# Seven block products in place of eight in part of the down projections of a two-FFN encoder block

## The chip, the cores and the metric

The kernel runs on one core of a Trainium2 chip. The metric is the device time of one execution, in microseconds; three runs of the kernel before gave 2103.3 to 2103.77 us, median 2103.62 us. The core has a matrix engine (TensorE, PE in the rows below), a vector engine (DVE), a scalar engine (ACT), GpSimd (POOL), a queue engine that issues transfers (SP), and 16 DMA engines.

## The reference, cut to what matters

```python
def swiglu(h, w_gate, w_up, w_down):
    return (jax.nn.silu(h @ w_gate) * (h @ w_up)) @ w_down

x = x + 0.5 * swiglu(rms_norm(x, norm_ffn1), ffn1_w_gate, ffn1_w_up, ffn1_w_down)
...   # mixer: sparse attention and a gated MLP on h = rms_norm(x)
x = x + 0.5 * swiglu(rms_norm(x, norm_ffn2), ffn2_w_gate, ffn2_w_up, ffn2_w_down)
```

x is 256 rows (SEQ) by 2048 columns (D_MODEL), the feed-forward width D_FF is 5632, everything float32. The down projection is therefore a product of 256 x 5632 with 5632 x 2048, and it occurs twice, once in each feed-forward block.

## The kernel before, in words

Every product is a sum over k-tiles of 128. `gemm` (L230 to L284) takes 1024 output columns at a time. For each pair of k-tiles one transfer on SP's queue brings 1 MB of weights into a buffer `w` (three buffers). For each k-tile `split_to` (L226 to L228) makes two parts of the 128 x 1024 weights: ACT casts them to the short matmul format (`wh`, L227), and DVE subtracts that from the original (`wl`, L228). There are three buffers of each. The activations were split in the same way before (`hTh`, `hTl` for the hidden layer). TensorE then does, for each of two row tiles t and two column halves j, three matmuls of 512 columns into one PSUM bank: high by high (L279), low by high (L280), high by low (L281). That is 12 matmuls for a k-tile, 24 for a pair.

`ffn` (L376 to L403) runs 11 chunks of 512 feed-forward columns: gate and up products over 16 k-tiles, SiLU on ACT (L389), product on DVE (L391), then a transpose through the DMA engines (`turn`, L291 to L299: planes on ACT, a transposing transfer, a copy on DVE) and a split into `hTh`, `hTl`. After all 11 chunks the down projection runs in two halves of 1024 columns, each over all 44 k-tiles, into four banks, which L401 adds to the residual `xres` with factor 0.5.

Side work such as the transposes stands in a queue `pending`; `tick` emits one piece after each k-tile. The order of instructions on each engine is fixed when the program is built, by a scheduler that follows a modelled timeline and the priorities of the code; at run time each engine works through its own list in order and waits at each instruction for what it needs. SP's queue is such a list too: a weight transfer waits until its buffer is free, and everything behind it waits with it.

Of the kernel before, what the change touches and what calls it, by code (L numbers as in the profile page):

```python
# [21 lines left out]
P = 128  # L22
# [44 lines left out]
def block_kernel(ctx: ExitStack, tc: tile.TileContext, x, positions, norm_ffn1, ffn1_w_gate, ffn1_w_up,  # L67
# [4 lines left out]
    const = ctx.enter_context(tc.tile_pool(name="const", bufs=1))  # L72
    act = ctx.enter_context(tc.tile_pool(name="act", bufs=1))
    wraw = ctx.enter_context(tc.tile_pool(name="wraw", bufs=3))
    wsp = ctx.enter_context(tc.tile_pool(name="wsp", bufs=3))
    tmp = ctx.enter_context(tc.tile_pool(name="tmp", bufs=8))
    small = ctx.enter_context(tc.tile_pool(name="small", bufs=4))
    psA = ctx.enter_context(tc.tile_pool(name="psA", bufs=6, space=bass.MemoryType.PSUM))
# [4 lines left out]
    def uid(s):  # L83
        cnt[0] += 1
        return f"{s}_{cnt[0]}"

    def ttile(shape=None):
        return tmp.tile(shape or [P, 512], F32, tag="t", name=uid("t"))
# [7 lines left out]
    def trbank(shape):  # L96
        return psT.tile(shape, F32, tag="tr", name=uid("tr"))
# [4 lines left out]
    def later(*stages):  # L102
        pending.extend(stages)
# [122 lines left out]
    def split_to(hi, lo, src):  # L226
        nc.scalar.copy(hi, src)  # L227
        nc.vector.tensor_sub(lo, src, hi.bitcast(F32))  # L228

    def gemm(xh, xl, nk, load, widths, first=0, rate=1, lead=None):  # L230
# [52 lines left out]
            k0 += kg  # L283
        return banks  # L284

    def loader(wap, c0, ncol):
        def load(k0, kg, dst):
            nc.sync.dma_start(dst, wap[k0 * P:(k0 + kg) * P, c0:c0 + ncol].rearrange("(k p) c -> p k c", p=P))
        return load
# [23 lines left out]
    class Normed:  # L313
# [59 lines left out]
        def xl(self, k, t):  # L373
            return self.l[:, k, t * P:(t + 1) * P]

    def ffn(nrm, wg, wu, wd, after_chunk, first=0, lead=None):  # L376
        with tc.tile_pool(name=uid("ffn"), bufs=1) as pool:
            hTh = pool.tile([P, KF, S], F32R, name=uid("hTh"))
            hTl = pool.tile([P, KF, S], F32R, name=uid("hTl"))
            for fc in range(FF // 512):  # L380
                def load(k0, kg, dst, fc=fc):
                    for i, wap in enumerate((wg, wu)):
                        nc.sync.dma_start(dst[:, :, i * 512:(i + 1) * 512],
                                          wap[k0 * P:(k0 + kg) * P, fc * 512:(fc + 1) * 512].rearrange(
                                              "(k p) c -> p k c", p=P))
                b = gemm(nrm.xh, nrm.xl, KD, load, [512, 512], first=first if fc == 0 else 0, lead=lead if fc == 0 else None)
                for t in range(NT):
                    sg = ttile()
                    nc.scalar.activation(sg, b[t][0], AF.Silu, scale=nrm.rstd[:, t:t + 1])  # L389
                    hh = ttile()  # L390
                    nc.vector.scalar_tensor_tensor(hh, b[t][1], nrm.rstd[:, t:t + 1], sg,  # L391
                                                   op0=ALU.mult, op1=ALU.mult)
                    later(partial(turn_split, hTh[:, fc * 4:fc * 4 + 4, t * P:(t + 1) * P],
                                  hTl[:, fc * 4:fc * 4 + 4, t * P:(t + 1) * P], hh))
            for half in range(2):
                b = gemm(lambda k, t: hTh[:, k, t * P:(t + 1) * P], lambda k, t: hTl[:, k, t * P:(t + 1) * P],
                         KF, loader(wd, half * 1024, 1024), [512, 512])
                for t in range(NT):
                    for j in range(2):
                        xs = xres[:, t, (half * 2 + j) * 512:(half * 2 + j + 1) * 512]  # L400
                        nc.vector.scalar_tensor_tensor(xs, b[t][j], 0.5, xs, op0=ALU.mult, op1=ALU.add)  # L401
                        if t == NT - 1 or after_chunk is to_out:
                            after_chunk(half * 2 + j, t)  # L403


    n1 = Normed(0)
# [387 lines left out]
```

## Time and profile before

| | |
|---|---|
| median of three runs | 2103.62 us |
| the profiled execution, its own time | 2102.13 us |
| its span (first to last instruction) | 2100.4 us |
| TensorE busy | 2084.0 us (99%), 9318 matmuls |
| DVE busy | 1165.4 us (55%) |
| ACT busy | 1038.5 us (49%) |
| weights and other data moved | 426.09 MB, mean 203 GB/s |

The profile is of one execution. Busy time of TensorE counts each matmul from its start to its modelled end; matmuls overlap, so the distance between starts says more than the duration of one. In the rows, "idle before" is the time an engine stood still ahead of a group of instructions, and the arrow names what released it. Idle time of an engine that is not the bottleneck costs nothing by itself.

### The profile page before, as it was taken

To read this page: it belongs to the slowest core of one execution; us is meant where nothing else is said; L and a number is where in the kernel's file an instruction comes from. 1 tells how busy PE (TensorE), PEld (TensorE's weight loads), DVE (VectorE), ACT (ScalarE), POOL (GpSimd) and SP (SyncE) were. 2 spreads that over 40 slices of the span, in tenths; PEclk is the share of its full clock that TensorE was granted. 3 is DMA by queue.
4 is the path that set the end of the run, shared out by engine and by line. 5 is a ranking of instruction groups with operands and counts; after the bars stand their busy time and mean duration, and the time that the engine had idled before them with its cause. 6 is when DMAs were issued, how large, how long until landed. Compare 5 with 4: busy or idle time off the path is not lost.

```text
span 2100.4 us, 24401 instructions
## 1 busy us (share of the span) xinstructions
PE 2084.0 (99%) x9318; PEld 1732.7 (82%) x9318; DVE 1165.4 (55%) x1362; ACT 1038.5 (49%) x1208; POOL 31.7 (2%) x60
## 2 busy tenths in 40 slices
PE   8999999999999999999999999999999999999998
PEld 6888888888888898888888888888888888888887
DVE  6555555555455457887544467555555555554443
ACT  5554444544345366567444445665444454443333
POOL 1000000000000000210000000000000000000000
PEclk9999999999999999999999999999999999999999
DMA  7666666666566477586665567676666666665654
GB/s 244 192 202 220 199 209 202 201 217 202 190 203 206 168 226 201 182 240 176 209 204 186 197 199 222 204 230 202 214 204 199 209 196 217 209 199 192 220 188 133
DMA packets 251526, 426.09 MB, mean 203 GB/s; under 512 B 106664, under 2 KB 108768, under 8 KB 251408
## 3 DMA queue, kind: packets, MB, share of 16 engines
q1 hardware_dynamic: 250880, 423.29, 63.7%
q0 software_dynamic: 528, 1.23, 0.3%
q8 instruction: 73, 1.20, 0.2%
q14 instruction: 45, 0.37, 0.1%
HBM read 398.26 MB, written 2.10 MB: 191 GB/s over the span
## 4 chain that ended last, share of the span: by engine, by line
PE 53%; ACT 0%; DMA 0%; DVE 0%; issue 0%; DVEq 0%
PE acc L279 17%; PE acc L281 17%; PE acc L280 17%; PE tr L687 0%; DMA tu<-pl 0%; DVE xres L401 0%; ACT L664 0%; PE tr L646 0%; ACT wh L227 0%; DVE pTs L299 0%; ACT vs L664 0%; DVEq L790 0%; ACT lgs L626 0%; ACT yah L227 0%; ACT pl L295 0%
## 5 line engine op out<-in xcount | busy, mean ns | idle before, releaser
L228 DVE TENSOR_TENSOR wl<-w,wh 128x1024 fp32r<-128x1024 f32 (+2 forms) x768 | 918.8, 1202 | 762.5 <-ACT wh L227 755.7
L227 ACT CAST wh<-w 128x1024 fp32r<-128x1024 f32 (+2 forms) x768 | 792.7, 1036 | 972.9 <-PE acc L280 957.3
L279 PE MATMUL acc<-wh,xTh 128*128 128x512 f32 (+1 forms) x2080 | 807.1, 388 | 3.4 <-ACT wh L227 3.4
L280 PE MATMUL acc<-wh,xTl 128*128 128x512 f32 (+1 forms) x2080 | 804.9, 387 | 0.0
L281 PE MATMUL acc<-wl,xTh 128*128 128x512 f32 (+1 forms) x2080 | 690.2, 387 | 0.0
L279 PEld LDWEIGHTS acc<-wh,xTh 128*128 128x128 f32 x2080 | 391.1, 188 | 81.8 <-ACT wh L227 4.7
L280 PEld LDWEIGHTS acc<-wh,xTl 128*128 128x128 f32 x2080 | 391.2, 188 | 76.6
L281 PEld LDWEIGHTS acc<-wl,xTh 128*128 128x128 f32 x2080 | 388.8, 188 | 77.3 <-DVE wl L228 0.6
L279 PE MATMUL acc<-wh,hTh 128*128 128x512 f32 x704 | 273.9, 389 | 0.0
L280 PE MATMUL acc<-wh,hTl 128*128 128x512 f32 x704 | 273.9, 389 | 0.0
L281 PE MATMUL acc<-wl,hTh 128*128 128x512 f32 x704 | 240.8, 389 | 0.0
L280 PEld LDWEIGHTS acc<-wh,hTl 128*128 128x128 f32 x704 | 132.2, 188 | 27.5
L281 PEld LDWEIGHTS acc<-wl,hTh 128*128 128x128 f32 x704 | 132.2, 188 | 27.4
L279 PEld LDWEIGHTS acc<-wh,hTh 128*128 128x128 f32 x704 | 132.2, 188 | 27.3
L299 DVE COPY t<-tu 128x1024 uint16<-128x1024 uint16 x60 | 45.6, 760 | 94.9 <-DMA tu<-pl 94.9
L295 ACT COPY pl<-t 128x1024 uint16<-128x1024 uint16 x58 | 60.4, 1043 | 0.4 <-DVE t L744 0.4
L280 PE MATMUL acc<-wh,ml 128*128 128x512 f32 x128 | 49.8, 389 | 0.0
L279 PE MATMUL acc<-wh,mh 128*128 128x512 f32 x128 | 49.6, 389 | 0.0
L281 PE MATMUL acc<-wl,mh 128*128 128x512 f32 x128 | 41.2, 389 | 0.0
L389 ACT ACTIVATE t<-acc,rstd 128x512 f32<-128x512 f32 x44 | 29.9, 690 | 10.7 <-PE acc L281 10.6
L391 DVE SCALAR_TENSOR_TENSOR t<-acc,rstd,t 128x512 f32<-128x512 f32 x44 | 32.0, 750 | 2.7 <-ACT t L389 2.7
L228 DVE TENSOR_TENSOR hTl<-t,hTh 128x512 fp32r<-128x512 f32 x44 | 30.2, 686 | 0.0
(182 smaller groups left out, 759.8 us busy)
## 6 DMA issues: line engine op xcount, KB each, us to landing
w<-in_ffn_w_down SPq DMA_DIRECT2D x88, 1024.0 KB, 5.1
w<-in_ffn_w_gate SPq DMA_DIRECT2D x175, 512.0 KB, 3.8
w<-in_ffn_w_up SPq DMA_DIRECT2D x175, 512.0 KB, 4.7
w<-in_w_in SPq DMA_DIRECT2D x72, 1024.0 KB, 5.0
w<-in_w_out SPq DMA_DIRECT2D x16, 1024.0 KB, 5.4
w<-in_w_in SPq DMA_DIRECT2D x16, 552.0 KB, 3.7
w<-in_w_up_attn SPq DMA_DIRECT2D x8, 1024.0 KB, 5.3
w<-in_w_up_sgu SPq DMA_DIRECT2D x8, 1024.0 KB, 5.4
```

Of the source, the lines that this page charges most:

```text
L227: nc.scalar.copy(hi, src)
L228: nc.vector.tensor_sub(lo, src, hi.bitcast(F32))
L279: nc.tensor.matmul(o_, sh, whj, start=(k == 0), stop=False)
L280: nc.tensor.matmul(o_, sl, whj, start=False, stop=False)
L281: nc.tensor.matmul(o_, sh, wlj, start=False, stop=(k == nk - 1))
L295: nc.scalar.copy(planes, src.bitcast(U16).rearrange("p (c h) -> p h c", h=2))
L299: nc.vector.tensor_copy(dst.bitcast(U16).rearrange("p j (c h) -> p h j c", h=2), turned)
L389: nc.scalar.activation(sg, b[t][0], AF.Silu, scale=nrm.rstd[:, t:t + 1])
L391: nc.vector.scalar_tensor_tensor(hh, b[t][1], nrm.rstd[:, t:t + 1], sg, op0=ALU.mult, op1=ALU.mult)
```

## The change

The feed-forward width is cut into two parts of 6 and 5 chunks (`PARTS`). For each part the gate and up products of its chunks run, and then the down projection over that part's k-tiles only (24 and 20), in two halves of 1024 columns. Each half ends with the four additions to `xres`, so there are twice as many of them.

In a half the k-tiles go in pairs. Of the 12 pairs of a half of the first part four (numbers 0, 2, 4, 6), and of the 10 pairs of the second part's halves four and two, are computed with seven block products instead of eight. The blocks are two row tiles by two k-tiles of activations and two k-tiles by two column halves of weights. The function that does it, `gemm_seven`, forms four sums or differences of weight blocks on DVE (three into a tile `T`, one in place in `w`), splits three tiles of 1024 columns and one of 512, and issues 7 x 3 = 21 matmuls. The sums of activation blocks S1 to S4 are made once per chunk by `sum_chunk`, which runs through the `pending` queue. The products P1, P5, P6 and P7 belong to several output blocks; after the last such pair `early` adds them to `xres` in five steps through the same queue. P2 and P3 collect in the two banks of the pool that otherwise serves transposes, P4 and a plain bank C22 in the main pool. The other pairs are computed as before, with 24 matmuls. The pool of split weights gets four buffers instead of three, and a scratch area for GpSimd's transfers is set to 4096 bytes.

Over the program each feed-forward block has 44 pairs in its halves, 14 of them with seven products.

```diff
-    wsp = ctx.enter_context(tc.tile_pool(name="wsp", bufs=3))
+    wsp = ctx.enter_context(tc.tile_pool(name="wsp", bufs=4))
...
+    def split_wide(src):
+        n = src.shape[-1]
+        whi = wsp.tile([P, 1024], F32R, tag="wh", name=uid("wh"))
+        wlo = wsp.tile([P, 1024], F32R, tag="wl", name=uid("wl"))
+        split_to(whi[:, :n], wlo[:, :n], src)
+        return [(whi[:, o:o + 512], wlo[:, o:o + 512]) for o in range(0, n, 512)]
+
+    def gemm_seven(tpool, xs, sums, nk, load, seven, early):
...
+        def product(name, st, w):
+            (sh, sl), (wh, wl) = st, w
+            if name not in acc:
+                acc[name] = trbank([P, 512]) if name in ("P2", "P3") else bank()
+            first = done[name] == 0
+            done[name] += 1
+            last = done[name] == total[name]
+            nc.tensor.matmul(acc[name], sh, wh, start=first, stop=False)
+            nc.tensor.matmul(acc[name], sl, wh, start=False, stop=False)
+            nc.tensor.matmul(acc[name], sh, wl, start=False, stop=last)
...
+            w = wraw.tile([P, 2048], F32, tag="w", name=uid("w"))
+            load(2 * g, 2, w.rearrange("p (k c) -> p k c", k=2))
+            if g in seven:
+                A11, A12, A22 = xs(2 * g, 0), xs(2 * g + 1, 0), xs(2 * g + 1, 1)
+                S1, S2, S3, S4 = sums(g)
+                T = tpool.tile([P, 3 * 512], F32, tag="T", bufs=2, name=uid("T"))
+                B11, B12, B21, B22 = (w[:, i * 512:(i + 1) * 512] for i in range(4))
+                nc.vector.tensor_sub(T[:, 0:512], B12, B11)
+                nc.vector.tensor_sub(B12, B22, B12)
+                nc.vector.tensor_add(T[:, 512:1024], B12, B11)
+                b11, t3 = split_wide(w[:, 0:1024])
+                product("P1", A11, b11)
+                product("P7", S3, t3)
+                t1, t2 = split_wide(T[:, 0:1024])
+                product("P5", S1, t1)
+                product("P6", S2, t2)
+                nc.vector.tensor_sub(T[:, 1024:1536], B21, T[:, 512:1024])
+                b21, b22 = split_wide(w[:, 1024:2048])
+                product("P2", A12, b21)
+                product("P3", S4, b22)
+                t4, = split_wide(T[:, 1024:1536])
+                product("P4", A22, t4)
...
+            else:
+                for kk in range(2):
+                    k = 2 * g + kk
+                    B = split_wide(w[:, kk * 1024:(kk + 1) * 1024])
+                    for t, names in enumerate((("P2", "P3"), ("P4", "C22"))):
+                        for j, name in enumerate(names):
+                            product(name, xs(k, t), B[j])
...
+                            pending.extendleft(reversed(early(acc["P1"], acc["P5"], acc["P6"], acc["P7"])))
+                    tick()
+        return [[acc["P2"], acc["P3"]], [acc["P4"], acc["C22"]]]
...
+    PARTS = ((0, 6, (4, 4)), (6, 5, (4, 2)))
+    KP = 24
...
+            for f0, nf, nseven in PARTS:
...
+                def sum_chunk(fi, fulls, hSh=hSh, hSl=hSl):
+                    f, g = fulls[0], fulls[1]
+                    s_ = ttile([P, 4, P])
+                    nc.vector.tensor_add(s_[:, 0, :], g[:, 0, :], g[:, 1, :])
+                    nc.vector.tensor_sub(s_[:, 1, :], s_[:, 0, :], f[:, 0, :])
+                    nc.vector.tensor_sub(s_[:, 2, :], f[:, 0, :], g[:, 0, :])
+                    nc.vector.tensor_sub(s_[:, 3, :], f[:, 1, :], s_[:, 1, :])
+                    split_to(hSh[:, fi], hSl[:, fi], s_)
...
+                    if fi < ns:
+                        later(partial(sum_chunk, fi, fulls))
...
+                    def early(P1, P5, P6, P7, c0=c0):
...
+                        def one():
+                            q["1"], q["5"] = ttile(), ttile()
+                            nc.scalar.activation(q["1"], P1, AF.Copy, scale=0.5)
+                            nc.scalar.activation(q["5"], P5, AF.Copy, scale=0.5)
+                            nc.vector.tensor_add(x0, q["1"], x0)
+
+                        def two():
+                            q["2"] = ttile()
+                            nc.vector.scalar_tensor_tensor(q["2"], P6, 0.5, q["1"], op0=ALU.mult, op1=ALU.add)
+                            nc.vector.tensor_add(x1, q["2"], x1)
+
+                        def three():
+                            q["3"] = ttile()
+                            nc.vector.scalar_tensor_tensor(q["3"], P7, 0.5, q["2"], op0=ALU.mult, op1=ALU.add)
+
+                        def four():
+                            nc.vector.tensor_add(both, both, q["3"][:, None, :].to_broadcast([P, 2, 512]))
+
+                        def five():
+                            nc.vector.tensor_add(right, right, q["5"][:, None, :].to_broadcast([P, 2, 512]))
...
+                    b = gemm_seven(pool, xs, sums, nf * 4, loader(wd[f0 * 512:(f0 + nf) * 512, :], c0, 1024),
+                                   [2 * i for i in range(nseven[half])], early)
+                    for t in range(NT):
+                        for j in range(2):
+                            xs_ = xres[:, t, (half * 2 + j) * 512:(half * 2 + j + 1) * 512]
+                            nc.vector.scalar_tensor_tensor(xs_, b[t][j], 0.5, xs_, op0=ALU.mult, op1=ALU.add)
...
-    nc = bacc.Bacc("TRN2", target_bir_lowering=False, num_devices=1)
+    nc = bacc.Bacc("TRN2", target_bir_lowering=False, num_devices=1,
+                   dynamic_dma_scratch_size=4096)
```

Three places show how the instructions stand now. The first is TensorE in the first half of the first down projection: one k-tile of the kernel before. `acc` are the four banks, `wh` and `wl` the two parts of the weights.

```order
L279 MATMUL acc_3685<-wh_3803,hTh_122 128x512
L280 MATMUL acc_3685<-wh_3803,hTl_123 128x512
L279 MATMUL acc_3689<-wh_3803,hTh_122 128x512
L281 MATMUL acc_3685<-wl_3804,hTh_122 128x512
L280 MATMUL acc_3689<-wh_3803,hTl_123 128x512
L281 MATMUL acc_3689<-wl_3804,hTh_122 128x512
L279 MATMUL acc_3693<-wh_3803,hTh_122 128x512
L280 MATMUL acc_3693<-wh_3803,hTl_123 128x512
L281 MATMUL acc_3693<-wl_3804,hTh_122 128x512
L279 MATMUL acc_3697<-wh_3803,hTh_122 128x512
L280 MATMUL acc_3697<-wh_3803,hTl_123 128x512
L281 MATMUL acc_3697<-wl_3804,hTh_122 128x512
```

The same engine now, inside the third pair (one with seven products). The second matrix of each matmul is now a block of `hTh` or of a block sum `hSh`, and `tr` are P2 and P3.

```order
L319 MATMUL acc_2191<-wh_2287,hSh_124 128x512
L320 MATMUL acc_2191<-wh_2287,hSl_125 128x512
L319 MATMUL acc_2195<-wh_2287,hSh_124 128x512
L321 MATMUL acc_2179<-wl_2278,hTh_122 128x512
L321 MATMUL acc_2183<-wl_2278,hSh_124 128x512
L320 MATMUL acc_2195<-wh_2287,hSl_125 128x512
L319 MATMUL tr_2204<-wh_2298,hTh_122 128x512
L320 MATMUL tr_2204<-wh_2298,hTl_123 128x512
L321 MATMUL acc_2191<-wl_2288,hSh_124 128x512
L321 MATMUL acc_2195<-wl_2288,hSh_124 128x512
L319 MATMUL tr_2208<-wh_2298,hSh_124 128x512
L320 MATMUL tr_2208<-wh_2298,hSl_125 128x512
```

A k-tile was 12 matmuls on one split tile; now every split tile of 1024 columns feeds only 6, and T's last part (`wh_2308`, 512 columns) feeds 3. The pair ends after 21.

The second place is DVE a little later in the same half. Before, it has one subtraction per k-tile and the transposes of the last chunk:

```order
L228 TENSOR_TENSOR wl_3736<-w_3733,wh_3735 128x1024
L299 COPY t_3701<-tu_3704 128x2x512
L228 TENSOR_TENSOR wl_3752<-w_3733,wh_3751 128x1024
L228 TENSOR_TENSOR wl_3770<-w_3767,wh_3769 128x1024
L228 TENSOR_TENSOR hTl_123<-t_3701,hTh_122 128x4x128
L299 COPY t_3725<-tu_3728 128x2x512
L228 TENSOR_TENSOR wl_3786<-w_3767,wh_3785 128x1024
L228 TENSOR_TENSOR wl_3804<-w_3801,wh_3803 128x1024
```

Now, from the middle of pair 2 to pair 6. `w_2315` is the buffer of pair 3, `w_2349` of pair 4, `w_2427` of pair 6, which takes over the buffer of pair 3.

```order
L378 COPY t_2263<-tu_2266 128x2x512
L228 TENSOR_TENSOR wl_2309<-T_2273,wh_2308 128x512
L334 TENSOR_TENSOR w_2349<-w_2349 128x512
L228 TENSOR_TENSOR wl_2318<-w_2315,wh_2317 128x1024
L228 TENSOR_TENSOR hTl_123<-t_2263,hTh_122 128x4x128
L335 TENSOR_TENSOR T_2351<-w_2349 128x512
L228 TENSOR_TENSOR wl_2334<-w_2315,wh_2333 128x1024
L228 TENSOR_TENSOR wl_2356<-w_2349,wh_2355 128x1024
L342 TENSOR_TENSOR T_2351<-w_2349,T_2351 128x512
L228 TENSOR_TENSOR wl_2366<-T_2351,wh_2365 128x1024
L228 TENSOR_TENSOR wl_2377<-w_2349,wh_2376 128x1024
L333 TENSOR_TENSOR T_2429<-w_2427 128x512
```

The block sums (L333, L334, L335, L342) stand between the splits. The last reader of pair 3's buffer is `wl_2334`, and the first instruction that needs pair 6's weights, L333, stands four instructions behind the release.

The third place is DVE where the first half ends and the second begins. Before:

```order
L228 TENSOR_TENSOR wl_4458<-w_4455,wh_4457 128x1024
L228 TENSOR_TENSOR wl_4489<-w_4455,wh_4488 128x1024
L401 SCALAR_TENSOR_TENSOR xres<-acc_3685,xres 128x512
L401 SCALAR_TENSOR_TENSOR xres<-acc_3689,xres 128x512
L401 SCALAR_TENSOR_TENSOR xres<-acc_3693,xres 128x512
L401 SCALAR_TENSOR_TENSOR xres<-acc_3697,xres 128x512
L228 TENSOR_TENSOR wl_4518<-w_4515,wh_4517 128x1024
```

Now (`w_2657` and `T_2659` are pair 0 of the second half, `w_2743` pair 2):

```order
L333 TENSOR_TENSOR T_2745<-w_2743 128x512
L334 TENSOR_TENSOR w_2743<-w_2743 128x512
L548 SCALAR_TENSOR_TENSOR xres<-tr_2204,xres 128x512
L228 TENSOR_TENSOR wl_2689<-w_2657,wh_2688 128x1024
L335 TENSOR_TENSOR T_2745<-w_2743 128x512
L548 SCALAR_TENSOR_TENSOR xres<-tr_2208,xres 128x512
L548 SCALAR_TENSOR_TENSOR xres<-acc_2216,xres 128x512
L548 SCALAR_TENSOR_TENSOR xres<-acc_2235,xres 128x512
L228 TENSOR_TENSOR wl_2701<-T_2659,wh_2700 128x512
L342 TENSOR_TENSOR T_2745<-w_2743,T_2745 128x512
L228 TENSOR_TENSOR wl_2711<-w_2708,wh_2710 128x1024
```

The four additions to `xres` (L401 before, L548 now) stand among the splits and block sums of the next half's first pairs.

## Rows read from the trace of the kernel before

**Rows 1.** The page: span, and busy time of each engine, share, instructions.
```profile
span 2100.4 us, 24401 instructions
...
PE 2084.0 (99%) x9318; PEld 1732.7 (82%) x9318; DVE 1165.4 (55%) x1362; ACT 1038.5 (49%) x1208; POOL 31.7 (2%) x60
```

**Rows 2.** Waits: engine, line, releaser: us in total, times, longest.
```profile
ACT wh L227 <- PE acc L280: 957.3, 586, 4.0
DVE wl L228 <- ACT wh L227: 755.7, 549, 3.4
...
PE tr L328 <- DMA xres<-in_x: 4.2, 2, 3.4
...
PE acc L279 <- ACT wh L227: 3.4, 4, 1.1
```

**Rows 3.** Windows inside the first down projection: length, PE busy (matmuls), clock, DMA.
```profile
500.00:600.00 100.00, 100.00 (x443) 1.00 0.57 195
600.00:700.00 100.00, 100.00 (x443) 1.00 0.63 208
```

**Rows 4.** Timeline of DVE in the first down projection: start, length, instruction [idle].
```profile
504.84 0.76 DVE L299 COPY t<-tu 128x1024 uint16<-128x1024 uint16 x1
505.49 2.34 DVE L228 TENSOR_TENSOR wl<-w,wh 128x1024 fp32r<-128x1024 f32 x2
...
515.35 1.22 DVE L228 TENSOR_TENSOR wl<-w,wh 128x1024 fp32r<-128x1024 f32 x1 [2.18 <-ACT wh L227]
518.07 1.22 DVE L228 TENSOR_TENSOR wl<-w,wh 128x1024 fp32r<-128x1024 f32 x1 [1.50 <-ACT wh L227]
```

**Rows 5.** Groups of one shape: count | busy us, mean ns | idle before.
```profile
L228 DVE TENSOR_TENSOR wl<-w,wh 128x1024 fp32r<-128x1024 f32 x736 | 895.9, 1223 | 742.5 <-ACT wh L227 741.5
...
L227 ACT CAST wh<-w 128x1024 fp32r<-128x1024 f32 x736 | 772.5, 1053 | 955.1 <-PE acc L280 940.6 <-DVE bias L539 3.3 <-ACT mh L227 2.0
...
L391 DVE SCALAR_TENSOR_TENSOR t<-acc,rstd,t 128x512 f32<-128x512 f32 x44 | 32.0, 750 | 2.7 <-ACT t L389 2.7
L228 DVE TENSOR_TENSOR hTl<-t,hTh 128x512 fp32r<-128x512 f32 x44 | 30.2, 686 | 0.0
...
L744 DVE TENSOR_TENSOR t<-sg,sg 128x512 f32<-128x512 f32 x8 | 5.3, 683 | 0.0
...
L453 DVE TENSOR_TENSOR q<-t,t 128x128 f32<-128x128 f32 x4 | 1.1, 283 | 0.0
```

**Rows 6.** Timeline of DVE at the second block's change of halves.
```profile
1974.41 2.48 DVE L401 SCALAR_TENSOR_TENSOR xres<-acc,xres 128x512 f32<-128x512 f32 x4
```

**Rows 7.** Timeline of DVE early on: L199 needs the result of L198.
```profile
27.67 0.39 DVE L198 TENSOR_SCALAR t<-t 128x480 f32<-128x480 f32 x1
28.10 0.66 DVE L199 TENSOR_TENSOR t<-t,t 128x480 f32<-128x480 f32 x1
```

**Rows 8.** Transfers of down weights: the page's row (KB each, us to landing).
```profile
w<-in_ffn_w_down SPq DMA_DIRECT2D x88, 1024.0 KB, 5.1
```

**Rows 9.** The same transfers between 540 and 600 us, apart.
```profile
L288 SPq DMA_DIRECT2D w<-in_ffn_w_down x11: 367/368/368, 543.8 to 598.2; - x11
...
DMA to landing us min/median/max: 4.7/4.8/5.2
```

**Rows 10.** The same between 612 and 640 us, apart.
```profile
L288 SPq DMA_DIRECT2D w<-in_ffn_w_down x5: 368/372/380, 614.5 to 639.2; - x5
...
DMA to landing us min/median/max: 5.0/5.1/6.3
```

**Rows 11.** Timeline at the end: DVE's last group, then SP's transfers of the output.
```profile
2093.45 2.48 DVE L401 SCALAR_TENSOR_TENSOR xres<-acc,xres 128x512 f32<-128x512 f32 x4 [4.71 <-PE acc L281]
2094.17 2.12 SPq L429 DMA_DIRECT2D out<-xres  x4
```

**Rows 12.** Windows around the first mixer products: length, PE busy (matmuls), clock, DMA.
```profile
720.00:750.00 30.00, 28.91 (x151) 1.00 0.57 160
750.00:780.00 30.00, 28.66 (x167) 1.00 0.73 206
```

More of the change, by code (lines that the diff above doesn't have):

```diff
@@ L284, in gemm @@
         return banks
+    def split_wide(src):
[5 more added lines that the diff above has]
+    def gemm_seven(tpool, xs, sums, nk, load, seven, early):
+        acc = {}
+        total = {}
+        np_ = nk // 2
+        for name in ("P1", "P5", "P6", "P7"):
+            total[name] = len(seven)
+        for name in ("P2", "P3", "P4"):
+            total[name] = len(seven) + 2 * (np_ - len(seven))
+        total["C22"] = 2 * (np_ - len(seven))
+        done = {k: 0 for k in total}
+        def product(name, st, w):
[8 more added lines that the diff above has]
+            nc.tensor.matmul(acc[name], sh, wl, start=False, stop=last)
+        left = len(seven)
+        wait = None
+        for g in range(np_):
+            w = wraw.tile([P, 2048], F32, tag="w", name=uid("w"))
[20 more added lines that the diff above has]
+                product("P4", A22, t4)
+                left -= 1
+                if left == 0:
+                    wait = 2
+            else:
[5 more added lines that the diff above has]
+                            product(name, xs(k, t), B[j])
+                    if wait is not None:
+                        wait -= 1
+                        if wait == 0:
+                            pending.extendleft(reversed(early(acc["P1"], acc["P5"], acc["P6"], acc["P7"])))
+                    tick()
+        return [[acc["P2"], acc["P3"]], [acc["P4"], acc["C22"]]]
@@ L374, in xl @@
             return self.l[:, k, t * P:(t + 1) * P]
+    PARTS = ((0, 6, (4, 4)), (6, 5, (4, 2)))
+    KP = 24
     def ffn(nrm, wg, wu, wd, after_chunk, first=0, lead=None):
         with tc.tile_pool(name=uid("ffn"), bufs=1) as pool:
[L378 to L394, printed above, removed]
```

51 lines of the change are left out of this document (42 added, 9 removed).

## The prediction

> **What bounds the kernel now.** I read first the busy times, then the waits, then the down projections by windows and DVE's timeline. TensorE is busy 2084.0 of 2100.4 us, DVE 55%, ACT 49% [rows 1]. The waits say the same: ACT stood 957.3 us until a matmul gave back a buffer of split weights, and DVE 755.7 us until ACT had cast; TensorE's own longest entries are 4.2 and 3.4 us [rows 2]. In the down projection, where the change is made, TensorE is busy all of 500 to 700 us at granted clock 1.00 (2.4 GHz), with 443 matmuls in each 100 us [rows 3]. A k-tile has 12 matmuls, and DVE's subtractions, which follow the release of buffers, come every 2.72 us (at 515.35 and 518.07, for instance) [rows 4]: 2.72 / 12 = 0.2267 us per matmul, 441 in 100 us, which agrees with the count (the ends of a window are counted twice). So here time is the number of matmuls times 0.2267 us, as long as the splits arrive in time. In each k-tile DVE has 1.50 us free and works 1.22 [rows 4].
>
> **What the change takes away.** A pair of k-tiles has 24 matmuls, a pair with seven products 21. With 14 such pairs in each of two feed-forward blocks that is 28 x 3 = 84 matmuls, the difference of the two lists of TensorE (9205 and 9121 rows). All stood in stretches without a gap, so 84 x 0.2267 = **19.04 us** go, unless TensorE then waits.
>
> **What it adds on DVE and ACT.** A 1024-column subtraction lasts 1.22 us, but two in a row took 2.34 [rows 4]: the second begins 1.12 after the first. In the same way four additions of 512 from PSUM took 2.48 us [rows 6], 0.60 apart and 0.68 for the last. Where an instruction needs its forerunner's result the overlap is gone: L199 began at 28.10, after 27.67 + 0.39 = 28.06 [rows 7]. A block sum of 512 columns has no row; the nearest is a sum of two SBUF tiles of that shape, 683 ns [rows 5]. It costs 0.60 in a row of others and 0.72 behind its own input; I take 0.60, since the order puts a split between most dependent sums, and keep the full durations as the other end.
>
> - A pair with seven products: 3 splits of 1024 (3 x 1.12), one of 512 (0.60), 4 block sums (2.40): 6.36 us on DVE, for 21 x 0.2267 = 4.76 us of TensorE. It is DVE-bound by itself.
> - The plain pair behind it: 2 x 1.12 = 2.24 us for 24 x 0.2267 = 5.44 us.
> - The two together: DVE 8.60 us, TensorE 10.20 us. At full durations (1.223, 0.686, 0.683 [rows 5]): 3.67 + 0.69 + 2.73 + 2.45 = 9.54 us. Still below 10.20.
> - ACT in the two: five casts of 1.05 us and one of 512 (about 0.6): 5.9 us. Not the bound.
>
> The Trainium skill, "VectorE: DVE Perf Modes", section Terms, says that the next DVE instruction can't issue until the pipe of the one before has emptied. By that the full durations and 9.54 us would hold; rows 4 and 6 show instructions starting 0.1 us earlier than that.
>
> **The wait that is added.** L333 waits for a weight transfer, in DVE's list ahead of splits that TensorE needs sooner (behind it stand the rest of the block sums and the last split of the pair before, and P4 waits for that). The order shows how late it comes: pair 3's buffer is released by `wl_2334`, SP then issues pair 6's transfer, and DVE has 1.12 + 0.60 + 1.12 + 1.12 = 3.96 us of work before L333. The transfer takes 5.1 us [rows 8]. So DVE stands 1.1 us per pair with seven products (0.7 at 4.7 us [rows 9], 2.3 at the longest, 6.3 [rows 10]). 8.60 + 1.1 = 9.7 us against 10.20: the double pair still fits, by 0.5 us.
>
> There is also a lead to start from. With four buffers a split is started when a buffer comes free and is ready 1.05 + 1.22 = 2.3 us later [rows 5], while TensorE still has three k-tiles, 8.16 us, before it: 5.9 us ahead. Inside a pair with seven products the three buffers ahead hold as little as 6 + 6 + 3 = 15 matmuls, 3.4 us, so the lead shrinks to 1.1 us and a little more, but stays above zero.
>
> **The smaller edits.**
> - First half of each part: two products (750 ns each [rows 5], 0.65 with the overlap), two copies (0.65 [rows 4]) and two splits (0.60) for the last chunk, 3.8 us of DVE, fall into the first double pair. The kernel before has them in the same place; the lead of 5.9 us takes them.
> - Change of halves: four additions of 0.60 [rows 6] stand among the first pair's splits. P1, P7, P5, P6 (12 matmuls, 2.72 us) need none of what is behind them but `wl_2689`, which follows the first addition: 0.68 + 1.12 = 1.8 us. Covered. Eight more such additions per block are hidden in the same way, or, behind the last half of a part, beside the next product.
> - `early`: four instructions of 0.60 and two of 1.12, 4.6 us over five k-tiles with 1.50 us free each. Hidden; in a stretch without free time it would cost up to 0.9 us per k-tile.
> - `sum_chunk`: four sums of 128 columns (283 ns [rows 5]) and a split of 512, 1.8 us, once in 16 k-tiles. Hidden.
> - Transfers: the same bytes; the DMA engines are 57 to 63% busy [rows 3], and two pairs now take 10.2 instead of 10.9 us.
> - End: the last half ends with the same four additions and four output transfers [rows 11]. Nothing.
> - Four buffers of splits elsewhere, and the smaller scratch area: between 720 and 780 us TensorE has 1.09 + 1.34 = 2.4 us of gaps [rows 12], so a gain of at most that; a loss could come only where an order is now less lucky, and I set the same 2.4 us. I take 0.
>
> **Sum.** For waits of TensorE I take 0.6 us over all eight halves, the low end of 0 to what the rivals below give, because the double pair fits at the median transfer. 2102.13 (the profiled execution, 2100.4 of it span) - 19.04 + 0.6 = 2083.7 us. The median of the runs shown is 2103.62, 1.5 us above that execution, and the runs of the changed kernel should stand as high: **2085.2 us**.
>
> **Rivals.**
>
> *DVE keeps its full durations and transfers land a little late* (5.6 us, between median and longest). The double pair then costs 9.54 + 5.6 - 4.35 (the 3.96 at full durations) = 10.8 us, 0.6 more than TensorE has. 28 x 0.6 = 17, less an estimated 1.5 us of lead used up in each of 8 halves (of the 5.9 most is needed inside the pairs): 5 us in place of my 0.6. Time 2089. For it: the overlap of DVE instructions is seen only with operands that were ready. Against it: [rows 4, 6], and 11 transfers with a median of 4.8 us where nothing else moved [rows 9].
>
> *The transfer becomes the bound*, the slower side. If every transfer for a pair with seven products lands after 6.3 us, as one of five did beside other traffic [rows 10], DVE stands 6.3 - 4.35 = 1.95 us there at full durations: 11.5 us per double pair, 1.3 too much. 28 x 1.3 = 36, less 12 of lead: 24 us, more than the 19.04 saved, so 2085.2 - 0.6 + 24 = 2109. It decides from about 6.1 us. For it: buffers now come free unevenly, and a transfer can overlap its neighbour or a transpose. Against it: half idle DMA engines [rows 3], and gaps between issues that stay near 5 us on average.
> The Trainium skill, "DMA: Bandwidth & Descriptors", section Bandwidth, gives 6.15 us for a transfer of 1 MB issued from GpSimd. By that figure this rival would hold; the transfers here go through SP and took 4.7 to 5.2 us when alone [rows 9].
>
> *The fourth buffer also closes the gaps elsewhere* [rows 12]: 2.4 us more and no wait of its own, 2082. For it: a longer lead helps where ACT and DVE have bursts. Against it: the waits there are on transposes and on small matmuls as much as on splits.
>
> That the change doesn't do what it says is ruled out by the order: 84 matmuls fewer.
>
> **Chances.** Forecast 0.68 (2083 to 2088), late splits 0.17 (2088 to 2098), transfer the bound 0.06, gaps closed 0.09. The range 2082 to 2096 leaves out the slow rival, the upper part of the first and what lies below the last. 0.2% is 4.2 us, about what a measurement of this kernel can tell from no change: faster means below 2099.4. Forecast, gaps closed and most of the first rival: 0.91 faster; 0.04 the same; 0.05 slower.
>
> **What would show it.** Right: 84 matmuls fewer; windows in the plain and the seven pairs alike with TensorE at 100% and 0.2267 us between starts; DVE near 85 to 95% busy in the first 40 us of a half, with waits of about 1 us before L333 on the transfer; TensorE waiting for `wl` under 2 us in total. Wrong, first rival: waits of L321 on DVE's L228 of 6 us or more in sum. Wrong, second: waits of L333 on transfers above 2 us, passed on to L321, and a landing above 6 us. Wrong in the sum itself: a distance between starts other than 0.2267 us in pairs with seven products, or gaps in the mixer that were not there.

## The result and the profile after

The changed kernel took 2079.23 us (median of four runs, 2077.48 to 2080.16) against 2103.46 us for the kernel before on the same chip (four runs, 2102.41 to 2103.77): ratio 0.9885, interval 0.9868 to 0.9902, a gain of 24.2 us. The forecast was 2085.2 us, with a range of 2082 to 2096. The direction and the main term were right; the gain is 6.0 us larger than forecast and lies outside the range. The profiled execution took 2080.16 us, 21.97 less than the one before (2102.13).

The page's first rows, for the changed kernel; they answer to [rows 1]:

```profile
span 2078.4 us, 24744 instructions
...
PE 2064.1 (99%) x9234; PEld 1717.6 (83%) x9234; DVE 1346.8 (65%) x1674; ACT 1095.3 (53%) x1296; POOL 30.2 (1%) x60
```

84 matmuls fewer (9318 to 9234), DVE 181 us busier, ACT 57. The waits of the changed kernel, to be read beside [rows 2] (engine, line, releaser: us in total, times, longest):

```profile
ACT wh L227 <- PE acc L280: 569.2, 360, 4.6
DVE wl L228 <- ACT wh L227: 535.7, 428, 3.8
...
DVE T L333 <- DMA w<-in_ffn_w_down: 12.0, 9, 2.2
...
PE acc L279 <- ACT wh L227: 1.3, 2, 0.9
...
PE tr L793 <- DVE s L389: 0.9, 1, 0.9
```

TensorE has no entry for L319, L320 or L321, the lines of the new function: it waits for nothing there. DVE does stand at L333 for a transfer, as forecast, but only nine times, 12 us in all. The wait of L279 for a split has gone from 3.4 to 1.3 us.

The first four double pairs of the first half by windows (length, then busy time and instructions of PE, PEld, DVE, ACT, POOL, granted clock, DMA share, GB/s); the row answers to [rows 3]:

```profile
278.10:318.90 40.80, 40.80 (x182) 33.78 (x181) 37.21 (x44) 27.46 (x32) 0.00 (x0) 1.00 0.69 219
```

Four double pairs are 4 x 45 = 180 matmuls, and 180 x 0.2267 = 40.8 us: TensorE is busy all of the 40.80. DVE is busy 91%, within the forecast 85 to 95%. DVE's timeline in that stretch, beside [rows 4, 6, 7] (start, length, instruction, idle before and its releaser):

```profile
301.54 0.69 DVE L333 TENSOR_TENSOR T<-w 128x512 f32<-128x512 f32 x1 [0.84 <-DMA w<-in_ffn_w_down]
302.26 0.69 DVE L334 TENSOR_TENSOR w<-w 128x512 f32<-128x512 f32 x1
302.87 0.68 DVE L228 TENSOR_TENSOR wl<-T,wh 128x512 fp32r<-128x512 f32 x1
303.47 0.68 DVE L335 TENSOR_TENSOR T<-w 128x512 f32<-128x512 f32 x1
304.07 1.22 DVE L228 TENSOR_TENSOR wl<-w,wh 128x1024 fp32r<-128x1024 f32 x1
305.21 0.68 DVE L342 TENSOR_TENSOR T<-w,T 128x512 f32<-128x512 f32 x1
```

A block sum starts 0.60 us after an instruction it does not depend on (302.87 to 303.47), and a split of 1024 gives way after 1.14 (304.07 to 305.21). That is the overlap taken from the kernel before (0.60 and 1.12). L334 after L333 starts 0.72 later; it overwrites the block that L333 reads. The groups of one shape (count | busy us, mean ns | idle before) and the page's row for the transfer, beside [rows 5, 8]:

```profile
L333 DVE TENSOR_TENSOR T<-w 128x512 f32<-128x512 f32 x28 | 19.3, 688 | 12.3 <-DMA w<-in_ffn_w_down 12.0
...
w<-in_ffn_w_down SPq DMA_DIRECT2D x88, 1024.0 KB, 5.2
```

**Where the time went, by stage.** Spans from landmarks of the two traces (first matmul of a stage to that of the next), us:

| | before | after |
|---|---|---|
| first feed-forward block, first mixer products | 798.4 | 786.7 |
| of it the first mixer product (the one with 368-column matmuls) | 51.67 | 48.93 |
| middle of the mixer | 393.4 | 393.4 |
| end of the mixer | 174.1 | 174.1 |
| second feed-forward block | 717.9 | 708.3 |
| last matmul's start to the end | 6.0 | 5.3 |

The second block loses 9.5 us, which is 42 x 0.2267. The other block has the same 42 matmuls less, and 2.7 us more went in the first mixer product, which the diff does not touch; 0.7 went at the very end. (9.5 and 2.7 are 12.2, and the row has 11.7: 0.4 more went in small pieces, and 0.9 came back at the start of the run, which the last section shows.) Each of the two has its rows below.

The row for the middle of the mixer hides a gain. In this execution TensorE stands there once, the 0.9 us at L793 in the waits above. In the second profile of the same kernel (`e0_again`, below) that wait is missing and the middle takes 392.25 us. The three traces with three buffers (before, `e7_scratch_only`, `e2_three_buffers`) have 393.4 to 393.8 there, nine of the ten with four buffers 392.2 to 392.8; this one is the exception. So about 1.2 us more go there, and in this execution they came back. Why the wait comes in one execution and not in the other is open.

The windows around the first mixer product, which answer to [rows 12]:

```profile
720.00:750.00 30.00, 29.58 (x168) 28.31 (x168) 16.60 (x29) 19.39 (x34) 1.53 (x3) 1.00 0.71 184
750.00:780.00 30.00, 30.00 (x172) 29.04 (x172) 19.03 (x36) 17.81 (x32) 1.60 (x2) 1.00 0.81 260
```

The idle time there is 0.42 us instead of 2.43. The end, on DVE and SP, beside [rows 11]:

```profile
2071.45 1.37 DVE L548 SCALAR_TENSOR_TENSOR xres<-tr,xres 128x512 f32<-128x512 f32 x2 [6.75 <-PE tr L321]
2072.81 1.37 DVE L548 SCALAR_TENSOR_TENSOR xres<-acc,xres 128x512 f32<-128x512 f32 x2
```
```profile
2072.16 2.37 SPq L576 DMA_DIRECT2D out<-xres  x4
```

Before, the four additions ran in 2.48 us, one behind the other. Now they take 2.73 us, because each waits for its own bank and the banks are done 0.68 us apart. TensorE's list shows why. Its last matmuls in the kernel before:

```profile
2092.80 0.39 PE L279 MATMUL acc<-wh,hTh 128*128 128x512 f32 x1
2093.02 0.61 PE L281 MATMUL acc<-wl,hTh 128*128 128x512 f32 x2
2093.48 0.39 PE L280 MATMUL acc<-wh,hTl 128*128 128x512 f32 x1
2093.70 0.39 PE L281 MATMUL acc<-wl,hTh 128*128 128x512 f32 x1
...
2094.38 0.39 PE L281 MATMUL acc<-wl,hTh 128*128 128x512 f32 x1
```

and in the changed kernel:

```profile
2071.70 0.39 PE L321 MATMUL tr<-wl,hTh 128*128 128x512 f32 x1
2071.93 0.39 PE L319 MATMUL acc<-wh,hTh 128*128 128x512 f32 x1
2072.15 0.39 PE L320 MATMUL acc<-wh,hTl 128*128 128x512 f32 x1
2072.38 0.39 PE L321 MATMUL acc<-wl,hTh 128*128 128x512 f32 x1
```

Before, the products with `wl` stand behind the `wh` products of other banks, so the first bank is done late (DVE starts at 2093.45, 0.93 us ahead of TensorE's last start), and DVE's queue of additions outlasts TensorE. Now the banks end in turn, 3 x 0.2267 = 0.68 apart, DVE starts 1.61 us ahead of TensorE's last start (2073.06), and 0.7 us of the tail is gone. The additions end 1.12 us behind that start and not 1.55 (2093.45 + 2.48 before, 2072.81 + 1.37 now), which is 0.43 of it; the rest lies behind them, in the output transfers.

### The profile page after: what moved, and what is told of

Read it like the earlier page. It is cut to its first block, busy times and chain, and to the rows that moved or that the text cites. A ratio compares the mean times of both kernels' runs of the same rounds, so it can differ in the third digit from the quotient of the medians.

```text
span 2078.4 us, 24744 instructions
## 1 busy us (share of the span) xinstructions
PE 2064.1 (99%) x9234; PEld 1717.6 (83%) x9234; DVE 1346.8 (65%) x1674; ACT 1095.3 (53%) x1296; POOL 30.2 (1%) x60
## 4 chain that ended last, share of the span: by engine, by line
PE 52%; DMA 0%; ACT 0%; DVE 0%; issue 0%; ACTq 0%
PE acc L281 14%; PE acc L280 14%; PE acc L279 14%; PE acc L320 2%; PE acc L319 2%; PE acc L321 2%; PE tr L320 2%; PE tr L321 2%; PE tr L319 2%; DMA tu<-pl 0%; PE tr L834 0%; DVE xres L548 0%; ACT L811 0%; PE tr L793 0%; ACT wh L227 0%
## 5 line engine op out<-in xcount | busy, mean ns | idle before, releaser
L279 PE MATMUL acc<-wh,xTh 128*128 128x512 f32 (+1 forms) x2080 | 806.7, 388 | 1.3 <-ACT wh L227 1.3
L281 PE MATMUL acc<-wl,xTh 128*128 128x512 f32 (+1 forms) x2080 | 782.6, 387 | 0.0
L279 PEld LDWEIGHTS acc<-wh,xTh 128*128 128x128 f32 x2080 | 391.0, 188 | 78.9 <-ACT wh L227 2.0
L281 PEld LDWEIGHTS acc<-wl,xTh 128*128 128x128 f32 x2080 | 390.0, 188 | 77.2
L319 PE MATMUL acc<-wh,hTh 128*128 128x512 f32 x296 | 115.1, 389 | 0.0
L320 PE MATMUL acc<-wh,hTl 128*128 128x512 f32 x296 | 115.1, 389 | 0.0
L321 PE MATMUL acc<-wl,hTh 128*128 128x512 f32 x296 | 104.6, 389 | 0.0
L319 PE MATMUL tr<-wh,hTh 128*128 128x512 f32 x268 | 104.3, 389 | 0.0
L320 PE MATMUL tr<-wh,hTl 128*128 128x512 f32 x268 | 104.3, 389 | 0.0
L321 PE MATMUL tr<-wl,hTh 128*128 128x512 f32 x268 | 92.7, 389 | 0.0
L320 PEld LDWEIGHTS acc<-wh,hTl 128*128 128x128 f32 x296 | 55.6, 188 | 11.5
L319 PEld LDWEIGHTS acc<-wh,hTh 128*128 128x128 f32 x296 | 55.6, 188 | 11.5
L321 PEld LDWEIGHTS acc<-wl,hTh 128*128 128x128 f32 x296 | 55.6, 188 | 11.5
L320 PEld LDWEIGHTS tr<-wh,hTl 128*128 128x128 f32 x268 | 50.3, 188 | 10.4
```

The costliest lines, as they stand in the source:

```text
L279: nc.tensor.matmul(o_, sh, whj, start=(k == 0), stop=False)
L281: nc.tensor.matmul(o_, sh, wlj, start=False, stop=(k == nk - 1))
L319: nc.tensor.matmul(acc[name], sh, wh, start=first, stop=False)
L320: nc.tensor.matmul(acc[name], sl, wh, start=False, stop=False)
L321: nc.tensor.matmul(acc[name], sh, wl, start=False, stop=last)
```

## The experiments

All were timed against the kernel before, whose medians in the three sets were 2103.11, 2103.1 and 2102.99 us.

**The changed kernel once more** (`e0_again`, no edit).

> The changed kernel once more, unchanged, to see how much of its gain is the spread of runs. The count of matmuls alone (84 x 0.2267 = 19.0 us) says 2084 against 2103.5; count plus the 2.4 us that its trace lacks between the first block and the scores and 0.7 us at the end says about 2081; if the first four runs are typical, 2079 (24 us).

2078.47 us (2077.97 to 2078.94), ratio 0.9882, interval 0.9867 to 0.9897. The first result stands. Both sets of runs together lie near 2078.8, which stands for the changed kernel in what follows.

**The fourth buffer and the scratch area alone**, in the kernel before.

```diff
-    wsp = ctx.enter_context(tc.tile_pool(name="wsp", bufs=3))
+    wsp = ctx.enter_context(tc.tile_pool(name="wsp", bufs=4))
...
-    nc = bacc.Bacc("TRN2", target_bir_lowering=False, num_devices=1)
+    nc = bacc.Bacc("TRN2", target_bir_lowering=False, num_devices=1, dynamic_dma_scratch_size=4096)
```

> The kernel before with four buffers of split weights instead of three (and the smaller scratch area, without which it does not fit). If the fourth buffer closes the gaps at the start of the mixer, TensorE's gaps between 720 and 780 us go from 2.4 us to about 0.4 and the time is 2 us lower, 2101.5. If the gaps closed for another reason (the order at the end of the second part), it stays at 2103.5 with 2.4 us of gaps.

2099.99 us (2098.6 to 2100.84), ratio 0.9984, interval 0.9976 to 0.9993: 3.1 us less without a matmul saved. By stages it is 1.6 us in the first mixer product, 0.8 in the middle of the mixer (392.57) and 0.7 at the end; 0.7 came back in its profiled execution through a later start. The tail is 5.3 us, as in the changed kernel. The first mixer product takes 50.08 us, with one gap of TensorE left. Its gaps between 745 and 765 us in the kernel before, and in this one between 735 and 786:

```profile
749.97 0.45 PE L279 MATMUL acc<-wh,xTh 128*128 128x368 f32 x1 [1.09 <-ACT wh L227]
751.48 0.43 PE L279 MATMUL acc<-wh,xTh 128*128 128x368 f32 x1 [0.21 <-ACT wh L227]
761.92 0.43 PE L279 MATMUL acc<-wh,xTh 128*128 128x368 f32 x1 [1.13 <-ACT wh L227]
```
```profile
755.13 0.43 PE L279 MATMUL acc<-wh,xTh 128*128 128x368 f32 x1 [1.60 <-ACT wh L227]
```

2.43 us of visible gaps became 1.60, but the product became 1.59 us shorter. It has the same 288 matmuls of 368 columns in both, with no other matmul between them. Without the gaps it takes 51.67 - 2.43 = 49.24 us before and 50.08 - 1.60 = 48.48 here: 0.8 us of the delay never showed as idle time. A matmul's row is longer than the distance between starts (0.39 against 0.2267 at 512 columns), so a start that comes a little late only shortens the overlap. The lists built for four buffers also have another order there (on TensorE, ACT and SP), so what the longer lead gives and what the order gives are not told apart.

**The scratch area alone.**

```diff
-    nc = bacc.Bacc("TRN2", target_bir_lowering=False, num_devices=1)
+    nc = bacc.Bacc("TRN2", target_bir_lowering=False, num_devices=1, dynamic_dma_scratch_size=4096)
```

> The kernel before, three buffers of splits, with the scratch area of GpSimd's transfers set to 4096 bytes and nothing else. Theory (the fourth buffer alone gives the 3.2 us that the kernel before with both edits gained): as the kernel before, 2103.1 us, between 2102.4 and 2103.9; first mixer product 51.7 us from its first 368-column matmul to the first of the next product. Rival (the scratch area gives it): 2099.9 us and 50.1.

2102.72 us (2102.23 to 2103.46), ratio 0.9998, interval 0.9989 to 1.0008; first mixer product 51.54, tail 6.0. The scratch area does nothing that shows; the 3 us are the fourth buffer's.

**Two parts, without any pair of seven products.**

```diff
-    PARTS = ((0, 6, (4, 4)), (6, 5, (4, 2)))
+    PARTS = ((0, 6, (0, 0)), (6, 5, (0, 0)))
...
-                ns = max(nseven)
+                ns = max(1, *nseven)
...
-                    if fi < ns:
+                    if fi < max(nseven):
```

> The changed kernel with the two parts and four buffers, but no pair with seven products (no block sums, no early additions). If the gain is matmuls and closed gaps, this keeps only the closed gaps and the shorter end: 2100.5 to 2101.5. If cutting the width in parts itself costs (four more ends of halves per block), 2104 or more; if it gains by itself what the sum lacked (5 us), 2098.

2099.91 us (2098.2 to 2101.08), ratio 0.9983, interval 0.9974 to 0.9992. First mixer product 50.06, tail 5.3, second block 717.9 as in the kernel before. The cut into parts, with twice as many additions to `xres`, costs nothing; what is gained is the fourth buffer's.

**The changed kernel with three buffers.**

```diff
-    wsp = ctx.enter_context(tc.tile_pool(name="wsp", bufs=4))
+    wsp = ctx.enter_context(tc.tile_pool(name="wsp", bufs=3))
```

> The changed kernel with three buffers of split weights. Inside a pair with seven products only two buffers of 6 and 3 matmuls (2.0 us) then lie ahead of a split that takes 2.3 us. If TensorE lives on that lead, it waits some 0.3 to 1 us at each of the 28 pairs: 8 to 28 us more, 2088 to 2107. If the lead does not matter there, it is within 2 us of the changed kernel, 2080, with only the mixer gaps back (2.4 us).

2090.2 us (2089.09 to 2093.75), ratio 0.994, interval 0.9927 to 0.9952: 11.4 us lost against the changed kernel. Its TensorE waits:

```profile
PE acc L279 <- ACT wh L227: 3.9, 6, 1.4
...
PE tr L321 <- DVE wl L228: 2.1, 4, 0.9
```

The first mixer product is back at 52.19 us and the tail at 6.0, 3.9 us together. The second block, where nothing but the pairs matters, takes 710.4 us instead of 708.3: the pairs with seven products do need the longer lead, but lose only some 2 us per block without it. So the time lies in the expected 2088 to 2107, but the pairs give some 4 us of the 11.4 and not 8 to 28.

**One extra sum of 512 columns on DVE per pair with seven products; then three.** The sum goes into a place that is overwritten before it is read.

```diff
                 nc.vector.tensor_add(T[:, 512:1024], B12, B11)
+                for _ in range(1):      # 3 in the other kernel
+                    nc.vector.tensor_add(T[:, 1024:1536], B12, B11)
```

> The same with one more block sum: 9.2 us per double pair. With 1.1 us of wait 10.3, just over 10.20: 0 to 3 us more, 2079 to 2082. Without it: no difference, 2079.

> The changed kernel with three more block sums of 512 columns in each pair with seven products (into the part of T that is overwritten later; results as before). DVE's double pair goes from 8.6 to 10.4 us against 10.20 of TensorE. If a wait of 1.1 us on the transfer stands on top as I worked out: 1.3 us too much, 28 times, less 12 of lead: 24 us more, 2103. If the wait on the transfer is absorbed: 0 to 6 us more, 2079 to 2085.

One: 2079.79 us (2078.76 to 2080.34), ratio 0.9889, interval 0.9874 to 0.9903; no change that stands clear of the runs of the changed kernel (2077.48 to 2080.16), and no wait of TensorE in L319 to L321. Three: 2102.61 us (2100.86 to 2104.09), ratio 0.9998, interval 0.9988 to 1.0007; all the gain is lost. At the prices with overlap a double pair costs DVE 8.60 + 0.60 = 9.2 us with one more sum and 8.60 + 1.80 = 10.4 with three, against TensorE's 10.20: the limit lies between, where those prices put it. At full durations one extra sum would already stand at 9.54 + 0.68 = 10.2 us, with the waits for transfers on top, and should have cost something.

The prices of the pairs alone do not give the size of the loss with three: 0.2 us too much, 28 times, is 5.6. DVE also has other work in these stretches: in the changed kernel it was busy 37.21 us in the window of four double pairs, which at 8.60 each are 34.4, so 0.7 more per double pair. With that three sums are 0.9 too much, an estimate of 25 us less what the lead takes. The expectation had 2103 for a wait of 1.1 us at each L333 on top; the number came out, the reason did not, for L333 waited only 4.0 us in all.

The waits with three:

```profile
PE acc L319 <- ACT wh L227: 10.3, 6, 3.6
...
PE tr L321 <- DVE wl L228: 3.0, 2, 1.5
PE tr L319 <- ACT wh L227: 1.1, 5, 0.2
...
DVE T L333 <- DMA w<-in_ffn_w_down: 4.0, 10, 1.1
```

and its windows (columns as in the windows above), with two matmuls out of the second window:

```profile
300.00:320.00 20.00, 18.16 (x72) 14.20 (x71) 18.07 (x23) 11.03 (x14) 0.00 (x0) 0.91 0.50 172
306.60:309.90 3.30, 3.30 (x9) 2.51 (x9) 3.30 (x4) 2.62 (x3) 0.00 (x0) 0.50 0.49 200
685.50:692.20 6.70, 4.04 (x10) 3.13 (x11) 6.31 (x10) 6.28 (x9) 0.00 (x0) 0.50 0.64 177
2044.00:2050.70 6.70, 5.47 (x13) 4.06 (x14) 6.67 (x9) 4.69 (x6) 0.00 (x0) 0.50 0.55 171
```
```profile
307.13 0.63 PE L320 MATMUL acc<-wh,hTl 128*128 128x512 f32 x1
307.56 0.63 PE L321 MATMUL acc<-wl,hTh 128*128 128x512 f32 x1
```

TensorE waits 14.4 us, 9.4 less than the 23.8 lost. The granted clock explains most of the rest. It is 0.91 on the mean of 300 to 320 us, the stretch of the first stall, and 0.996 over the run; in three stretches it stands at 0.50, which is 1.2 instead of 2.4 GHz, and there the matmuls start 0.43 us apart and not 0.2267. 2 x 0.4% of 2102 is 17 us at that clock. In the three windows, 16.7 us of it, TensorE is busy 12.8 us, so some 6 us are lost that way, an estimate; the last 3 us show in no wait.

**Pairs with seven products next to each other**, with no plain pair between. The odd pairs use their neighbour's block sums, so the numbers are not the reference's; the work is the same.

```diff
-                                   [2 * i for i in range(nseven[half])], early)
+                                   list(range(nseven[half])), early)
```

> The same number of pairs with seven products, but next to each other (0, 1, 2, 3 of a half) and not every other one; the odd pairs use the block sums of their neighbour, so the numbers computed there are not the reference's. Same matmuls. If DVE's 6.4 us for 4.76 us of TensorE counts, four in a row lack 6.4 us, less a lead of some 3: 3 us in each of six halves and little in the two with two pairs: about 20 us more, 2099. If DVE has more room than I worked out, it stays near 2079.

2092.6 us (2089.94 to 2094.88), ratio 0.9951, interval 0.9934 to 0.9967: 13.8 us lost. DVE in the first 20 us of the half (columns as above):

```profile
278.00:298.00 20.00, 18.69 (x81) 14.66 (x80) 19.82 (x25) 14.10 (x18) 0.00 (x0) 1.00 0.53 171
```

DVE is busy 19.82 of 20 us and TensorE runs dry: in the whole run it waits 7.4 us in L319 to L321. The loss is less than the 20 us expected. A pair with seven products is DVE-bound by itself, as worked out (6.36 us against 4.76); the plain pair behind it pays the debt.

**Eighteen pairs of 44 instead of fourteen.**

```diff
-    PARTS = ((0, 6, (4, 4)), (6, 5, (4, 2)))
+    PARTS = ((0, 6, (5, 5)), (6, 5, (4, 4)))
```

> Seven products in 18 of 44 pairs (five in each half of the first part, four in each of the second): 8 pairs and 24 matmuls less than the changed kernel, 24 x 0.2267 = 5.4 us. If TensorE still never waits: 2078.8 - 5.4 = 2073.4. If DVE is at its end in a longer run of such pairs, the gain is eaten: 2076 to 2079.

2074.69 us (2073.16 to 2075.37), ratio 0.9864, interval 0.9849 to 0.9879: the best version here, 4.1 us below the changed kernel where 24 matmuls are 5.44 us. DVE stands 23.1 us at L333, and TensorE now waits a little (L321 on DVE, 0.8 us in all).

**Seven products only in the first parts; and nowhere in the last halves.** These look for the 1.1 us by which the first mixer product is shorter in the changed kernel (48.93) than with the fourth buffer alone (50.08).

```diff
-    PARTS = ((0, 6, (4, 4)), (6, 5, (4, 2)))
+    PARTS = ((0, 6, (4, 4)), (6, 5, (0, 0)))      # the other: (6, 5, (4, 0))
...   # and the two edits around ns, as with two parts alone
```

> Seven products in four pairs of each half of the first part, none in the second part: 16 pairs in the program, 48 matmuls fewer than before, 48 x 0.2267 = 10.88 us. Theory (the 1.1 us by which the first mixer product is shorter in the changed kernel than with the fourth buffer alone come from the seven-product pairs of the part that runs just ahead of it, which shift the transposes): that product takes 50.1 us, and the time is 2099.9 - 10.9 = 2089.0. Rival (it comes with seven products anywhere): 48.9 us, and 2087.9.

> As the changed kernel, but the last half of each block has no pairs with seven products: 24 pairs, 72 matmuls fewer, 16.32 us. Theory (the two such pairs of the last half shorten the first mixer product by 1.1 us): 50.1 us for it, and 2099.9 - 16.3 = 2083.6. Rival (the half before it does): 48.9 us, and 2082.5.

2087.11 us (2085.86 to 2087.55), ratio 0.9923, interval 0.9908 to 0.9938, and 2081.41 us (2081.08 to 2081.69), ratio 0.9898, interval 0.9881 to 0.9914. The first mixer product took 48.63 and 48.84 us: the rival, with times about 1 us below the rival's. The pairs just ahead of it have nothing to do with it. From shortly ahead of that product to its middle the instructions stand in the same order on TensorE, DVE, ACT and SP in the kernel with parts only and in the one with seven products in the first parts. What differs is one transposing transfer. SP issues it, and ACT, which has casts queued behind its copy, waits for it. The kernel with parts only, SP and then ACT:

```profile
744.60 1.23 SPq L425 DMA_TRANSPOSE tu<-pl  x1
```
```profile
749.51 0.78 ACT L429 COPY t<-tu 128x512 uint16<-128x512 uint16 x1 [1.91 <-DMA tu<-pl]
```

Seven products in the first parts:

```profile
740.01 1.23 SPq L425 DMA_TRANSPOSE tu<-pl  x1
```
```profile
743.57 0.78 ACT L429 COPY t<-tu 128x512 uint16<-128x512 uint16 x1 [0.56 <-DMA tu<-pl]
```

From issue to the copy that it releases: 4.91 us there, 3.56 here. It is 4.72 with the fourth buffer alone and 3.34 in the changed kernel, and 3.3 to 3.9 in all eight traces with four buffers and pairs of seven products. TensorE's gap follows the copy one for one. Counted from the first 368-column matmul, the copy starts after 13.9 to 14.3 us in those eight traces, and TensorE's gap is 0.13 to 0.49 us; with parts only and with the fourth buffer alone it starts after 15.3 and 15.4 us, and the gap is 1.56 and 1.60.

What sets those two apart can be read in their DMA queues: between the transfer's issue and its landing one packet of 16 KB runs on the queue that the profile calls `instruction`. In the other eight no such packet falls there. The row for it with parts only (746.5 to 749.5 us) and with the fourth buffer alone (745.9 to 750.7; packets, MB, share of 16 engines):

```profile
q8 instruction: 1, 0.02, 2.4%
```
```profile
q8 instruction: 1, 0.02, 1.5%
```

With parts only it runs from 747.26 to 748.42 us; the transfer's own packets of 256 bytes are through at 747.5, and the copy starts 2.0 us later. With seven products in the first parts they are through at 743.1, and the copy starts 0.5 us later. So the 1.1 us hang on where that packet falls in the run, which the change shifts without aiming at it: luck, as far as ten traces can show it, since no run moves the packet alone. It is not all that makes such a transfer late: the one before it took 6.4 us with parts only, with no packet of that queue beside it.

## Why the prediction was off

**Right: the count.** 84 x 0.2267 = 19.04 us; each block lost its 42 matmuls at that price, with no gap between them.

**Right: DVE's prices and margin.** The overlap prices hold in the trace (0.60, and 1.14 for 1.12), and the extra sums put the limit between 9.2 and 10.4 us, where they do. The wait at L333 on the transfer, 1.1 us per pair in the forecast, came nine times in 28, 12 us in all: mis-sized, harmless. The 0.6 us allowed for TensorE's waits over eight halves measured 0. The first rival, which rested on full durations, fell with those starts and with the one extra sum that cost nothing. The Trainium skill, "VectorE: DVE Perf Modes", section Terms, has the pipe empty before the next instruction issues. The starts 0.60 us apart at 0.68 duration disagree with that entry again, now for the block sums themselves.

**Wrong: "Four buffers of splits elsewhere ... a gain of at most that ... I take 0".** The fourth buffer alone gives 3.1 us, and 2.7 us of the changed kernel's gain lie in the first mixer product, 0.7 at the end and, where the wait at L793 is missing, 1.2 in the middle of the mixer. Three things were wrong with the step. The value taken, 0, was the wrong end: with the fourth buffer two of the three gaps are gone [rows 12]. The bound, 2.4 us, was read from idle time, and idle time misses delays that are shorter than the overlap of two matmuls; 0.8 us lay there, and the middle of the mixer was outside the windows read. And the transposing transfer that landed 1.4 us sooner, in what the diff leaves alone, was in no term; it was worth 1.1 us, and, as far as the traces show, it was luck. The third rival had the mechanism, with the same bound of 2.4 us, and was given a chance of 0.09.

**Wrong: "End: ... Nothing."** The end has the same additions and transfers, but the order built for four buffers finishes the banks one by one: 0.7 us, shown by the fourth buffer alone (tail 5.3) and by three buffers in the changed kernel (6.0).

**Wrong: "1.5 us above that execution, and the runs of the changed kernel should stand as high".** The changed kernel's profiled execution stood 0.9 us above its median. It has two delays that the second profile of the same kernel lacks, 0.9 us at the start of the run, below, and 1.2 in the middle of the mixer; that second execution took 2078.26 us. So the offset belonged to one execution and not to the kernel.

**The sum, by executions.** From 2102.13: 19.04 for the count, 2.74 for the first mixer product, 0.7 for the end, 0.4 in small pieces, less 0.9 for a later start: 21.97, to 2080.16. Against the forecast's 2083.7 that is 3.5 us, and the offset (+1.5 forecast, -0.9 measured) makes 2.4 more: the 6.0 us of the miss. To the second profile it is 23.87 us: 19.04, 2.74, 0.7, 1.2 for the middle of the mixer, and 0.2 in small pieces.

## What to carry to other kernels

On a TensorE-bound kernel, matmuls removed are worth their count times the distance between starts, as long as the engines that feed it have work for less than TensorE's time over the stretch that their buffers span, and not pair by pair. A buffer added to a shared pool acts in every stage that uses the pool and on the order that a scheduler builds: price it by a run of its own, and take idle time in the trace as the lower end of what it can give, not as the upper. Before an offset between one profiled execution and a median is carried over to another kernel, look for what makes executions differ.

## What the runs showed of the hardware

**The start.** After TensorE's early gaps the first matmuls of the program start 0.43 us apart, the distance that the kernel with three extra sums shows where its granted clock is 0.50 (1.2 GHz); then the distance falls to 0.2267. The granted clock of a window there reads 1.00, but it is no reading: the trace's record of the clock begins only with an entry at full speed, 14.31 us into the span in the kernel before, 16.07 in the changed kernel and 14.29 in its second profile. So when the clock rises differs from execution to execution. The kernel before:

```profile
13.37 0.63 PE L279 MATMUL acc<-wh,xTh 128*128 128x512 f32 x1
13.79 0.63 PE L280 MATMUL acc<-wh,xTl 128*128 128x512 f32 x1
...
14.62 1.17 PE L281 MATMUL acc<-wl,xTh 128*128 128x512 f32 x4
15.64 0.40 PE L279 MATMUL acc<-wh,xTh 128*128 128x512 f32 x1
```

The changed kernel:

```profile
14.80 1.75 PE L281 MATMUL acc<-wl,xTh 128*128 128x512 f32 x4
16.39 0.39 PE L279 MATMUL acc<-wh,xTh 128*128 128x512 f32 x1
```

The same four matmuls of L281 take 1.17 us and 1.75, and by the next L279 the second execution has lost 0.87 us on the first (5.00 against 5.87 from the first L279, at 10.64 and 10.52). The changed kernel's own second profile has the early form, so it is not the kernel.

**The clock after a stall.** With three extra sums TensorE's granted clock stood at 0.50 in three stretches, each behind a wait of TensorE of 1.5 or 1.6 us that ended at 304.66, 683.86 and 2041.49, and the loss was 9.4 us larger than its waits; with nine waits at L333 that never reached TensorE it stayed at 1.00.
